# Eight column tiles ahead of each norm, head sums with the squares as stationary operand, and operands moved by 32 bytes

## The chip, the cores and the metric

The kernel runs on one NeuronCore of a Trainium2 chip. The metric is the device time of one execution in microseconds (us). The names used for engines: PE is TensorE's matmul stream and PEld its weight loads, DVE is VectorE, ACT is ScalarE, POOL is GpSimd, SP is SyncE, which here only issues transfers. SBUF is the on-chip memory, PSUM the accumulator memory, whose banks hold 512 float32 columns.

## What is computed

Two different blocks of two layers each, one after the other, on 256 tokens of width 1024. The first block's layer is, cut to what matters here:

```python
def hybrid_layer(x, ...):
    h = rms_norm(x, norm1_g)
    proj = h @ w_in
    q, k, v, iq, ik, iw, a_in, c_in, g_in = jnp.split(proj, IN_SPLITS, axis=-1)
    q = partial_rope(rms_norm(q.reshape(B, S, N_HEADS, HEAD_DIM), q_norm_g), *rope_attn)
    k = partial_rope(rms_norm(k.reshape(B, S, N_KV_HEADS, HEAD_DIM), k_norm_g), *rope_attn)
    y_attn = dsa_attention(q, k, v, iq, ik, iw) @ w_attn_out
    a_val, a_gate = jnp.split(a_in, 2, axis=-1)
    a = causal_dwconv(a_val * jax.nn.sigmoid(a_gate), conf_conv_w) + conf_conv_b
    ...
    x = x + merged @ w_o
    u = causal_dwconv(rms_norm(x, norm2_g) @ w_up, ffn_conv_w) + ffn_conv_b
    u_gate, u_val = jnp.split(u, 2, axis=-1)
    return x + (jax.nn.silu(u_gate) * u_val) @ w_down
```

The second block works on 512 rows (the 256 tokens and 256 context rows z); it also normalizes its query and key heads (of 64 elements) by the root of their mean square.

## The kernel before

Everything lies transposed in SBUF: 128 features on the partitions, tokens along the columns, a vector of 1024 features as eight slices `k`. Each matrix product is made one column tile (128 outputs) at a time in split precision. `Kern.weights` (L71 to L85) loads a tile of 128 x 1024 weights on SP's queue, ACT rounds it to float32r (`whi`, L68), and DVE or POOL subtracts to get the rest (`wlo`, L69); the operand is split in the same way into `hh` and `hl`. `Kern.mm` (L94 to L103) then issues 24 matmuls into a PSUM bank: per slice `whi` x `hh` (L100) and `whi` x `hl` (L101), and after them the eight of `wlo` x `hh` (L103). In the first block each matmul streams 256 columns, in most of the second block 512. In the first block's projections every second weight tile's subtraction goes to POOL, as one instruction of 1024 columns.

Before a norm, `early` (L205 to L212) splits x times the gain without the root, as soon as a slice of x is there (`oph`, `opl`). `opening` (L230 to L248) runs the first column tiles on that operand: four at the first norm of a layer (tag n1), three at the second (n2), each in a bank of its own. After the first tile it issues the two matmuls of the mean square (`mean`, L182) and the root (`rms`, L185 to L196), then makes the normed operand slice by slice (L242 and `split`), and multiplies each finished tile in PSUM by the root (L244). The following tiles use the normed operand. The sums for the root come from `sq_add` (L158 to L176): ACT squares, DVE adds.

The tiles are consumed in pairs: after n1 by a tanh on ACT (L291) and a product on DVE (L292) for the 31-tap convolution, whose taps (L275) DVE works off between other work; after n2 by a bias on ACT (L608) and two taps on DVE (L610), then a product (L614). A bank is free for the next tile when its consumers are done. Instructions run in order on each engine, in an order that a scheduler sets when the kernel is built; SP issues the weight loads in their order, up to four tiles ahead.

The mean squares of the ten key and query heads (`sums`, L340): ACT squares a tile, and one matmul with a 128 x 32 matrix that has a column of ones at the head's place streams the 256 squares, so that ten matmuls add rows to one bank. `head_rms` (L359) copies the 32 rows to SBUF (L361), transposes them (L364) and takes the root on 64 columns. The second block does the same with `hot2` (L1290) and `head_norms` (L993 to L1004).

At the start, x comes in four transfers on two queues, then the vectors of layer 0 (245 KB), an identity, the table const1 (864 KB) and the weights.

## Time and profile before

| | |
|---|---|
| median of three runs | 2914.49 us (2914.34 to 2915.78) |
| the profiled execution's own time | 2914.19 us |
| its span (first to last instruction) | 2912.4 us |
| PE busy | 2845.2 us, 98% |
| DVE busy | 2123.3 us, 73% |
| ACT busy | 1336.4 us, 46% |
| POOL busy | 351.1 us, 12% |
| the first block, by its last weight tiles | up to about 1180 us |

Busy time is what an engine's instructions cover; matmuls are pipelined, so a matmul's own duration is longer than its distance to the next one, and it is the distance that adds up. The chain that ended last follows the work back from the end, at each step to what released it.

### The profile page before, as it was taken

The numbers are of one execution on the slowest core, as the hardware profiler recorded it, in microseconds if no ns is written. First come the engines' busy times: TensorE is split into PE (matmuls) and PEld (weight loads), VectorE is DVE, ScalarE is ACT, GpSimd is POOL, SyncE is SP. The second block draws the span as 40 slices with busy tenths as digits, with TensorE's granted clock in tenths as the row PEclk, the third lists the DMA queues.
The fourth block names the chain that finished last, engine by engine and source line by source line (L and its number), as shares of the span: only waits on it lengthen the run. The fifth ranks groups of instructions, "written<-read, shape, count | busy, mean of one in ns | idle before, by whom it ended". The sixth has DMA issues, their size and how long they took to land.

```text
span 2912.4 us, 47602 instructions
## 1 busy us (share of the span) xinstructions
PE 2845.2 (98%) x18738; PEld 2551.3 (88%) x18738; DVE 2123.3 (73%) x3809; ACT 1336.4 (46%) x2189; POOL 351.1 (12%) x204
## 2 busy tenths in 40 slices
PE   7999999999899999999999999999999999999999
PEld 7889999998899999888888679888888888877999
DVE  7999789889986898666777855766765444585654
ACT  5455666544546765433226464433234332365543
POOL 3333422033234210000000000000000000000000
PEclk9999999999999999999999999999999999999999
DMA  6445557654455567554552112544644445422455
GB/s 209 145 127 162 177 186 219 226 173 137 136 160 176 182 217 239 165 155 161 182 183 97 53 45 73 159 145 148 188 142 152 137 136 167 134 88 68 167 180 154
DMA packets 127936, 447.65 MB, mean 154 GB/s; under 512 B 14304, under 2 KB 19936, under 8 KB 127072
## 3 DMA queue, kind: packets, MB, share of 16 engines
q1 hardware_dynamic: 124672, 439.14, 47.4%
q10 hardware_dynamic: 3040, 5.48, 0.5%
q8 instruction: 147, 2.41, 0.3%
q14 instruction: 77, 0.63, 0.1%
HBM read 443.51 MB, written 1.05 MB: 153 GB/s over the span
## 4 chain that ended last, share of the span: by engine, by line
PE 87%; DVE 8%; ACT 2%; DMA 1%; issue 1%; POOL 0%; SPq 0%; ACTq 0%; DVEq 0%; POOLq 0%
PE mmb L100 26%; PE mmb L101 26%; PE mmb L103 25%; DVE wlo L69 2%; PE outb L980 1%; PE atb L947 1%; ACT whi L68 1%; PE mmb L110 1%; PE mmb L111 1%; PE mmb L109 1%; DVE opl L69 1%; DVE cvb L275 1%; DMA mraw<-in_w_mod_dram 1%; PE mmb L975 1%; PE atb L182 0%
## 5 line engine op out<-in xcount | busy, mean ns | idle before, releaser
L68 ACT ACTIVATE whi<-wraw 128x1024 fp32r<-128x1024 f32 (+1 forms) x688 | 715.7, 1042 | 946.1 <-PE mmb L101 792.8
L69 DVE TENSOR_TENSOR wlo<-wraw,whi 128x1024 fp32r<-128x1024 f32 (+1 forms) x575 | 698.9, 1217 | 232.8 <-ACT whi L68 187.8
L100 PE MATMUL mmb<-oph,whi 128*128 128x256 f32 x2512 | 635.0, 290 | 20.6 <-ACT whi L68 11.9
L101 PE MATMUL mmb<-opl,whi 128*128 128x256 f32 x2512 | 629.2, 287 | 5.2 <-DVE opl L69 3.0
L100 PE MATMUL mmb<-hh,whi 128*128 128x512 f32 (+1 forms) x1776 | 612.4, 357 | 1.1 <-ACT whi L68 1.1
L101 PE MATMUL mmb<-hl,whi 128*128 128x512 f32 (+1 forms) x1776 | 609.2, 355 | 0.0
L100 PEld LDWEIGHTS mmb<-oph,whi 128*128 128x128 f32 x2512 | 486.6, 194 | 34.4 <-ACT whi L68 13.7
L101 PEld LDWEIGHTS mmb<-opl,whi 128*128 128x128 f32 x2512 | 487.0, 194 | 13.2 <-DVE opl L69 4.8
L777 DVE SCALAR_TENSOR_TENSOR mjunk<-mraw,cvec 128x1024 f32<-128x1024 f32 x256 | 316.0, 1234 | 245.1 <-DMA mraw<-in_w_mod_dram 238.6
L100 PEld LDWEIGHTS mmb<-hh,whi 128*128 128x128 f32 x1776 | 336.0, 189 | 55.4 <-issue 8.0
L103 PE MATMUL mmb<-hh,wlo 128*128 128x512 f32 (+1 forms) x1776 | 379.3, 355 | 0.0
L101 PEld LDWEIGHTS mmb<-hl,whi 128*128 128x128 f32 x1776 | 335.9, 189 | 47.4 <-issue 1.9
L103 PE MATMUL mmb<-oph,wlo 128*128 128x256 f32 x2512 | 357.1, 285 | 0.0
L100 PE MATMUL mmb<-dh,whi 128*128 128x256 f32 (+1 forms) x1122 | 343.2, 328 | 1.8 <-ACT whi L68 1.7
L69 POOL TENSOR_TENSOR wlo<-wraw,whi 128x1024 fp32r<-128x1024 f32 x113 | 285.8, 2529 | 487.5 <-ACT whi L68 402.7
L101 PE MATMUL mmb<-dl,whi 128*128 128x256 f32 (+1 forms) x1122 | 341.9, 327 | 0.0
L103 PEld LDWEIGHTS mmb<-hh,wlo 128*128 128x128 f32 x1776 | 297.9, 189 | 46.7 <-issue 0.4
L103 PEld LDWEIGHTS mmb<-oph,wlo 128*128 128x128 f32 x2512 | 327.5, 193 | 0.2
L100 PEld LDWEIGHTS mmb<-dh,whi 128*128 128x128 f32 x1122 | 213.2, 190 | 21.0 <-ACT whi L68 2.4
L101 PEld LDWEIGHTS mmb<-dl,whi 128*128 128x128 f32 x1122 | 213.3, 190 | 18.2
L275 DVE SCALAR_TENSOR_TENSOR cvb<-u,vec,cvb 128x256 f32<-128x256 f32 x480 | 212.6, 481 | 3.6
L103 PE MATMUL mmb<-dh,wlo 128*128 128x256 f32 (+1 forms) x1122 | 209.1, 327 | 0.2 <-DVE wlo L69 0.2
(335 smaller groups left out, 2838.4 us busy)
## 6 DMA issues: line engine op xcount, KB each, us to landing
wraw<-in_w_ff_dram SPq DMA_DIRECT2D x208, 512.0 KB, 3.5
wraw<-in_w_in_dram SPq DMA_DIRECT2D x200, 512.0 KB, 3.6
mraw<-in_w_mod_dram SPq DMA_DIRECT2D x144, 512.0 KB, 4.1
wraw<-in_w_up_dram SPq DMA_DIRECT2D x88, 512.0 KB, 4.3
wraw<-in_w_y_dram SPq DMA_DIRECT2D x64, 512.0 KB, 3.6
wraw<-in_w_ff_dram SPq DMA_DIRECT2D x64, 448.0 KB, 3.8
wraw<-in_w_down_dram SPq DMA_DIRECT2D x32, 448.0 KB, 4.0
wraw<-in_w_down_dram SPq DMA_DIRECT2D x16, 512.0 KB, 4.6
```

The costliest lines, as they stand in the source:

```text
L68: nc.scalar.activation(hi, src, AF.Copy)
L69: (lo_eng or nc.vector).tensor_tensor(lo, src, hi.bitcast(F32), op=OP.subtract)
L100: nc.tensor.matmul(ps, hi[:, k], xh[:, k0 + k], start=start and k == 0, stop=False)
L101: nc.tensor.matmul(ps, hi[:, k], xl[:, k0 + k], start=False, stop=False)
L103: nc.tensor.matmul(ps, lo[:, k], xh[:, k0 + k], start=False, stop=stop and k == kt - 1)
L109: nc.tensor.matmul(ps, hi[:, k], a, start=start, stop=False)
L110: nc.tensor.matmul(ps, hi[:, k], b, start=False, stop=False)
L111: nc.tensor.matmul(ps, lo[:, k], a, start=False, stop=stop)
L275: nc.vector.scalar_tensor_tensor(box[0], u[:, j, t:t + S], V("cw", 31 * j + t), box[0], op0=OP.mult, op1=OP.add)
L777: nc.vector.scalar_tensor_tensor(junk, raw, 1.0, K.cvec[:, e], op0=OP.mult, op1=OP.mult, accum_out=K.mods[l][:, e, 8 * m + k:8 * m + k + 1])
L947: nc.tensor.matmul(ps[:, :n], self.q[:, self.pair, tb * P:(tb + 1) * P], self.kpad[:, self.key(e), self.keys[0]:self.keys[1]], start=True, ...
L975: nc.tensor.transpose(pt[:, s * P:(s + 1) * P], lg[:, e, s * P:(s + 1) * P], K.ident)
```

## The change

- `opening` takes eight column tiles at every norm of the first block, in n banks (four at n1, five at n2), so that banks hold two tiles side by side. The first two tiles run slices 0 to 6 first, with the root's matmuls behind the first (behind the second at the very start), and both slices 7 come after that. The normed operand is made between the multiplications of the following tiles.
- The head sums: the squares (128 features x 128 tokens) become the stationary operand, a single column of 1/1024 streams; the result has tokens on the partitions at once. The copy and the transposes go, and the root is taken on 20 columns. The second block does the same with a 128 x 2 matrix: two or four matmuls where there was one.
- `shifted`: the float32r operands of the first block and those of the last feed-forward start 8 elements (32 bytes) into their tiles, at an odd multiple of 32 bytes; they started at multiples of 512 bytes. The weight tiles stay where they were, and so do the operands that stream 512 columns.
- POOL's subtraction is cut into four instructions of two slices.
- At the start the gains of the first norm (4 KB) are loaded by themselves ahead of x, the first weight tile is loaded in two halves between the parts of x, ACT loads its table for the copies at once, the squares come after all of `early`, and the other constants wait until the norm is made. z and the second block's vectors are loaded later.

```diff
     def weights(self, src, kt=KD):
+        return self.ahead.pop() if self.ahead else self.load(src, kt)
+
+    def load(self, src, kt=KD, cut=KD):
...
-        nc.sync.dma_start(raw[:, :kt], src)
+        cuts = [slice(k, min(k + cut, kt)) for k in range(0, kt, cut)]
+        for c in cuts:
+            nc.sync.dma_start(raw[:, c], src[:, c])
...
+            if self.nsplit % of < share:
+                for c in cuts:
+                    nc.scalar.activation(hi[:, c], raw[:, c], AF.Copy)
+                for k in range(0, kt, 2):
+                    c = slice(k, min(k + 2, kt))
+                    nc.gpsimd.tensor_tensor(lo[:, c], raw[:, c], hi[:, c].bitcast(F32), op=OP.subtract)
+            else:
+                for c in cuts:
+                    self.split(hi[:, c], lo[:, c], raw[:, c])
...
-        def opening(gname, srcs):
-            banks = []
-            for i, src in enumerate(srcs):
...
+        def opening(gname, srcs, n):
+            banks = [K.bank() for _ in range(n)]
+            tiles = [banks[i % n][:, i // n * S:(i // n + 1) * S] for i in range(len(srcs))]
+            two = []
+            for i in range(2):
+                two.append(K.weights(srcs[i]))
+                K.mm(tiles[i], two[i], *K.early, ks=range(KD - 1))
+                if i == (l == 0 and gname == "n1"):
                     rb = K.rms()
...
+            for i in range(2):
+                K.mm(tiles[i], two[i], *K.early, ks=(KD - 1,))
+            def finish(i):
+                if i > 1:
+                    K.mm(tiles[i], K.weights(srcs[i]), *K.early)
+                nc.vector.tensor_tensor(tiles[i], tiles[i], rb, op=OP.mult)
+            finish(0)
+            finish(1)
+            hh, hl = operand()
+            for k in range(KD):
+                if k % 3 == 2:
+                    finish(2 + k // 3)
+                h = K.np.tile([P, S], F32, name="hn", bufs=3)
+                nc.vector.scalar_tensor_tensor(h, x[:, k], V(gname, k), rb, op0=OP.mult, op1=OP.mult)
+                act = K.split(hh[:, k], hl[:, k], h)
+            for i in range(4, len(tiles)):
+                finish(i)
+            K.imm = (K.imm + len(srcs) - n) % len(K.mmset)
+            return tiles, hh, hl, act
...
             def sums(j, sq):
-                nc.tensor.matmul(ssq[0:32, :S], K.onehot[:, j], sq, start=j == 0, stop=j == 9)
+                for b in range(2):
+                    nc.tensor.matmul(ssq[:, 10 * b + j:10 * b + j + 1], sq[:, b * P:(b + 1) * P], K.inv[:, 0:1],
+                                     start=True, stop=True)
...
-            first, hh, hl = opening("n2", [A["w_up"][l, i] for i in range(3)])
+            first, hh, hl, _ = opening("n2", [A["w_up"][l, i] for i in range(8)], 5)
...
+            dh = shifted(ff, [NF, S], name="dh")
+            dl = shifted(ff, [NF, S], name="dl")
...
+def shifted(pool, shape, **kw):
+    n, w = shape
+    t = pool.tile([P, n * w + 16], F32R, **kw)
+    return t[:, 8:8 + n * w].rearrange("p (a b) -> p a b", b=w)
```

The order of the instructions at three places. On ACT at the start of the program, before:

```order
L211 ACT_TABLE_LOAD
L211 ACTIVATE oph<-xz,vec_0_69 128x256
L68 ACTIVATE whi<-wraw 128x1024
L163 ACTIVATE nacc_87<-xz 128x256
L211 ACTIVATE oph<-xz,vec_0_69 128x256
L166 ACTIVATE nsq<-xz 128x256
```

and in the change (the lines are those of the changed file):

```order
L683 ACT_TABLE_LOAD
L683 ACTIVATE nwarm<-inv 128x1
L68 ACTIVATE whi<-wraw 128x512
L228 ACTIVATE oph<-xz,vec_0_69 128x256
L68 ACTIVATE whi<-wraw 128x512
L228 ACTIVATE oph<-xz,vec_0_69 128x256 x5
L90 ACTIVATE whi<-wraw 128x1024
L228 ACTIVATE oph<-xz,vec_0_69 128x256 x2
L180 ACTIVATE nacc_112<-xz 128x256
L183 ACTIVATE nsq<-xz 128x256 x4
```

The table load no longer waits for data, the squares stand behind all eight slices of `oph`, and the second weight tile is rounded before them.

On DVE at the second norm of the first layer, where the first tiles are consumed, before (mmb_4726, mmb_4801 and mmb_4833 are the three tiles made ahead, nry the root, uu0 and uu1 the two halves of a consumed pair):

```order
L244 TENSOR_TENSOR mmb_4833<-mmb_4833,nry_4761 128x256
L610 SCALAR_TENSOR_TENSOR uu0_4871<-mmb_4726,vec1_0_69,uu0_4871 128x255
L610 SCALAR_TENSOR_TENSOR uu1_4875<-mmb_4801,vec1_0_69,uu1_4875 128x255
L610 SCALAR_TENSOR_TENSOR uu0_4871<-mmb_4726,vec1_0_69,uu0_4871 128x254
L610 SCALAR_TENSOR_TENSOR uu1_4875<-mmb_4801,vec1_0_69,uu1_4875 128x254
```

and in the change (mmb_4905 to mmb_4909 are the five banks; mmb_4908 holds tile 3 alone and is the first that the ninth tile can take):

```order
L638 SCALAR_TENSOR_TENSOR uu1_5211<-mmb_4906,vec1_0_69,uu1_5211 128x255
L638 SCALAR_TENSOR_TENSOR uu1_5223<-mmb_4908,vec1_0_69,uu1_5223 128x255
L264 TENSOR_TENSOR mmb_4907<-mmb_4907,nry_4941 128x256
L638 SCALAR_TENSOR_TENSOR uu1_5211<-mmb_4906,vec1_0_69,uu1_5211 128x254
L638 SCALAR_TENSOR_TENSOR uu1_5223<-mmb_4908,vec1_0_69,uu1_5223 128x254
L642 TENSOR_TENSOR uu0_5207<-uu0_5207,uu1_5211 128x256
```

The multiplication of the last tile (mmb_4907, which waits for that tile's matmuls) now stands ahead of the last reading of mmb_4908.

On PE at the end of the query heads of the first layer, before:

```order
L103 MATMUL mmb<-oph,wlo 128x256 x8
L341 MATMUL cvb<-sq,const_306 32x256
L100 MATMUL mmb<-oph,whi 128x256
L341 MATMUL cvb<-sq,const_306 32x256
L101 MATMUL mmb<-opl,whi 128x256
```

and in the change:

```order
L120 MATMUL mmb<-oph,wlo 128x256 x8
L376 MATMUL cvb<-inv,sq 128x1 x2
L117 MATMUL mmb<-oph,whi 128x256
L118 MATMUL mmb<-opl,whi 128x256
L117 MATMUL mmb<-oph,whi 128x256
L118 MATMUL mmb<-opl,whi 128x256
L376 MATMUL cvb<-inv,sq 128x1 x2
```

Two one-column matmuls stand where one of 256 columns stood, and the transposes L364 that came some matmuls later are gone.

## Rows read from the trace of the kernel before

**Rows 1.** The page: engines, then the chain that ended last, by engine.

```profile
PE 2845.2 (98%) x18738; PEld 2551.3 (88%) x18738; DVE 2123.3 (73%) x3809; ACT 1336.4 (46%) x2189; POOL 351.1 (12%) x204
...
PE 87%; DVE 8%; ACT 2%; DMA 1%; issue 1%; POOL 0%; SPq 0%; ACTq 0%; DVEq 0%; POOLq 0%
```

**Rows 2.** A stretch: length, busy PE PEld DVE ACT POOL, PE's clock, DMA.

```profile
410.00:570.00 160.00, 158.69 (x1315) 157.90 (x1314) 144.60 (x233) 100.79 (x160) 26.86 (x22) 1.00 0.67 212
```

**Rows 3.** Timeline: start, us, engine, line, count [idle before], at the start.

```profile
7.48 1.28 ACT L211 ACT_TABLE_LOAD   x1 [7.48 <-DMA vec<-in_vec_dram]
8.78 0.51 ACT L211 ACTIVATE oph<-xz,vec 128x256 fp32r<-128x256 f32 x1
10.78 1.06 ACT L68 ACTIVATE whi<-wraw 128x1024 fp32r<-128x1024 f32 x1 [1.50 <-DMA wraw<-in_w_in_dram]
...
24.18 1.12 PE L103 MATMUL mmb<-oph,wlo 128*128 128x256 f32 x8
25.14 0.28 PE L100 MATMUL mmb<-oph,whi 128*128 128x256 f32 x1
```

**Rows 4.** The tile xz in the first 20 us: its loads.

```profile
DMA to landing us min/median/max: 4.1/4.8/5.4
```

**Rows 5.** Timeline of PE: the waits at the openings of the four norms.

```profile
32.45 0.39 PE L100 MATMUL mmb<-oph,whi 128*128 128x256 f32 x1 [1.39 <-ACT th L291]
35.41 0.38 PE L100 MATMUL mmb<-oph,whi 128*128 128x256 f32 x1 [1.27 <-ACT oph L68]
...
400.00 0.35 PE L100 MATMUL mmb<-oph,whi 128*128 128x256 f32 x1 [0.61 <-DVE xz L575]
...
597.22 0.39 PE L101 MATMUL mmb<-opl,whi 128*128 128x256 f32 x1 [1.61 <-DVE opl L212]
610.07 0.38 PE L100 MATMUL mmb<-oph,whi 128*128 128x256 f32 x1 [2.02 <-ACT th L291]
...
976.50 0.36 PE L100 MATMUL mmb<-oph,whi 128*128 128x256 f32 x1 [0.87 <-DVE xz L575]
```

**Rows 6.** Groups by line and shape: count, busy us, mean ns, idle before.

```profile
L244 DVE TENSOR_TENSOR mmb<-mmb,nry 128x256 f32<-128x256 f32 x14 | 5.7, 421 | 0.0
L610 DVE SCALAR_TENSOR_TENSOR uu<-mmb,vec,uu 128x254 f32<-128x254 f32 x88 | 41.2, 476 | 1.0
L69 DVE TENSOR_TENSOR wlo<-wraw,whi 128x1024 fp32r<-128x1024 f32 x479 | 594.9, 1243 | 182.0 <-ACT whi L68 156.7 <-PE mmb L103 20.6 <-PE atb L1092 2.0
L69 POOL TENSOR_TENSOR wlo<-wraw,whi 128x1024 fp32r<-128x1024 f32 x113 | 285.8, 2529 | 487.5 <-ACT whi L68 402.7 <-DVE cvb L275 22.5 <-PE mmb L103 10.6
L69 POOL TENSOR_TENSOR dl<-uu,dh 128x256 fp32r<-128x256 f32 x44 | 50.9, 1156 | 236.9 <-ACT dh L68 236.9
L69 DVE TENSOR_TENSOR opl<-mg,oph 128x256 fp32r<-128x256 f32 x16 | 18.6, 1161 | 5.3 <-ACT oph L68 5.1
L69 DVE TENSOR_TENSOR opl<-hn,oph 128x256 fp32r<-128x256 f32 x32 | 13.9, 478 | 0.0
```

**Rows 7.** Timeline of PE: the last head sums of the first layer.

```profile
120.85 0.39 PE L100 MATMUL mmb<-oph,whi 128*128 128x256 f32 x1
121.16 0.62 PE L341 MATMUL cvb<-sq,const 128*32 128x256 f32 x2
121.71 0.39 PE L101 MATMUL mmb<-opl,whi 128*128 128x256 f32 x1
...
125.00 0.41 PE L364 MATMUL atb<-ident,ssr 32*128 32x32 f32 x2 [2.20 <-DVE ssr L361]
```

**Rows 8.** Timeline of PE: float32 matmuls of 64 columns, in the second block.

```profile
2669.78 2.00 PE L980 MATMUL outb<-av,pT 128*128 128x64 f32 x16
2671.62 1.08 PE L947 MATMUL atb<-nkp,nq 128*128 128x512 f32 x2
```

**Rows 9.** Timeline of PE: float32r matmuls of 512 columns, in the second block.

```profile
2193.45 1.98 PE L103 MATMUL mmb<-hh,wlo 128*128 128x512 f32 x8
2195.27 0.39 PE L100 MATMUL mmb<-hh,whi 128*128 128x512 f32 x1
```

More of the change, by code (lines that the diff above doesn't have):

```diff
@@ L52, in __init__ @@
         self.imm = self.iat = 0
-        self.acc, self.last = {}, {}
+        self.acc, self.last, self.ahead = {}, {}, []
     @contextmanager
@@ L206, in early @@
     if k == 0:
-        K.early = (pool.tile([P, KD, S], F32R, name="oph", tag="op2h"),
-                   pool.tile([P, KD, S], F32R, name="opl", tag="op2l"))
+        K.early = (shifted(pool, [KD, S], name="oph", tag="op2h"),
+                   shifted(pool, [KD, S], name="opl", tag="op2l"))
     hh, hl = K.early
@@ L223, in operand @@
         def operand(pool=big, tag="op0"):
[L224 to L225 removed]
+            return (shifted(pool, [KD, S], name="oph", tag=tag + "h"),
+                    shifted(pool, [KD, S], name="opl", tag=tag + "l"))
         def w_in(j):
             return K.weights(A["w_in"][l, j], KD)
[L230 to L246 removed]
+        def opening(gname, srcs, n):
[6 more added lines that the diff above has]
+                if i == (l == 0 and gname == "n1"):
+                    rb = K.rms()
+            for i in range(2):
[17 more added lines that the diff above has]
+            return tiles, hh, hl, act
@@ L615, in first_layer @@
                 K.split(dh[:, j], dl[:, j], us[0], nc.gpsimd)
+                if j == 0 and l == DEPTH - 1:
+                    with tc.issue_after(act.ins):
+                        nc.scalar.dma_start(xz[:, :, S:], A["z"])
+                        for i in range(DEPTH):
+                            nc.scalar.dma_start(vec2[i], A["vec2"][i])
                 if j == 2:
@@ L693, in const1_array @@
     causal = np.concatenate([tri, np.zeros((P, P), np.float32), tri], axis=1)
-    onehot = np.zeros((P, 10, 32), np.float32)
-    for h in range(10):
-        onehot[:, h, h] = 1.0
-    return np.ascontiguousarray(np.concatenate([acos, asin, icos, isin, causal, onehot.reshape(P, 320)], axis=1))
+    return np.ascontiguousarray(np.concatenate([acos, asin, icos, isin, causal], axis=1))
 def ptile(w):
@@ L870, in feed_forward @@
         pad(ff, PAD_FF2)
-        dh = ff.tile([P, NF, T], F32R, name="dh")
-        dl = ff.tile([P, NF, T], F32R, name="dl")
+        dh = shifted(ff, [NF, T], name="dh") if T == S else ff.tile([P, NF, T], F32R, name="dh")
+        dl = shifted(ff, [NF, T], name="dl") if T == S else ff.tile([P, NF, T], F32R, name="dl")
         for j in range(NF):
@@ L1526, in two_blocks_kernel @@
         early(K, big, xz[:, :, :S], vec1[0], "n1", k)
+    for k in range(KD):
         K.sq_add(xz[:, k, :S], k)
```

103 lines of the change are left out of this document (37 added, 66 removed).

## The prediction

> **What bounds the kernel now.** I read the page first: PE is busy for 98% of the span, and the chain that ended last runs 87% through PE and 8% through DVE [rows 1]. So time can come from three places only: from fewer or shorter matmuls, from gaps between them, and from what lies ahead of the first one. The stretches show where a wait of PE is likely: in the feed-forward of the first layer (410 to 570 us) PE works without a pause at full clock, but DVE is busy for 144.6 of 160 us beside it [rows 2]; there DVE has a tenth to spare, and an added DVE instruction can reach PE. The timeline gives distances, which count more than durations: eight float32r matmuls of 256 columns begin at 24.18 and the next at 25.14, so one takes 0.12 us [rows 3]; eight of 512 columns take 1.82 us, 0.2275 each [rows 9]. The 256 further columns cost 0.1075 us, so 0.0125 us of each matmul does not depend on its length. A column tile of 24 matmuls takes 2.9 us. The openings show small waits of PE [rows 5], the last head sums one long wait [rows 7].
>
> **The start.** Now ACT waits until 7.48 us for the vectors, loads its table for 1.28 us, and waits again for weights until 10.78 us; the third column tile begins at 25.14 us [rows 3]. In the change the table is loaded beforehand, and x, whose transfers land 4.1 to 5.4 us after issue [rows 4], comes with the first weights, without 245 KB of vectors and 864 KB of constants in the way. I let ACT begin near 6 us. Up to the third tile's weights it does two halves of a weight tile (0.6 us each, an estimate from 1.06), eight slices of `oph` at 0.51 [rows 3], a weight tile, eight squares (at most as long as `oph`, the same shape), a table load and one more weight tile: 1.2 + 4.1 + 1.1 + 4.1 + 1.3 + 1.1 = 12.9 us, so the third tile begins near 18.9 instead of 25.1. The first two tiles fit before it. I take **-6** us; bounds -8 (squares faster, loads earlier) and -2 (the loads crowd each other).
>
> **The first norm (n1) of each layer.** PE waits 1.39 and 1.27 us in layer 0, 1.61 and 2.02 in layer 1 [rows 5], for the last slice, for a bank and for the normed operand. Eight tiles last 23 us, longer than the normed operand needs, and slice 7 is put off behind two tiles; both waits go. Late next is a bank: the ninth tile needs the bank of tiles 0 and 4, which is free after the third product on DVE, and in the order these products stand behind the multiplication of the eighth tile: 0.42 us [rows 6] and three products of about 0.48 (as the tap of the same size, [rows 6]), 1.9 us, of which six or seven matmuls of another tile fill 0.8. So 2.7 becomes 1.1 and 3.6 becomes 1.1: **-4** us; bounds -6 and 0.
>
> **The second norm (n2).** Here there is little to gain: 0.61 and 0.87 us [rows 5]. The order puts the multiplication of the eighth tile ahead of the last reading of the bank that the ninth tile takes: 0.42 + 2 x 0.48 = 1.4 us of wait. Then DVE has four consumed pairs in arrears, with a subtraction of 1.24 us per weight tile between them [rows 6], and the tenth and the twelfth tile wait about 1 us each. DVE also does 18 more multiplications over the four norms (32 instead of 14), 7.6 us, with a tenth of its time free [rows 2]. I put 3.2 us of waits against 0.7 at each of the two norms: **+5** us; bounds 0 and +10. Queued behind these DVE instructions are the subtractions of the next weight tiles, so PE would wait for `wlo` too.
>
> **Head sums.** A sum of 256 columns takes 0.55 us from its start to PE's next matmul [rows 7]. The new pair of matmuls streams one column, and its price is that of loading 128 x 128 float32 weights: not in the trace with one column; the nearest row is 64 columns, 16 records in 1.84 us, 0.115 each [rows 8]. A float32 product makes two records, so a head costs 4 x 0.115 = 0.46 us: 20 x 0.09 = -1.8 us. The transposes go, with the wait of 2.20 us for DVE's copy in layer 0 [rows 7] and 0.3 us of their own in each layer: -2.8. The root's chain is shorter by copy and transposes, which only moves the next wait earlier. Together **-4.6** us; bounds -7 and 0 (the wait reappears at the next transposes, for the same DVE). In the second block 48 small products of 0.23 us (11 us) stand for 14 long ones of about the same sum; 16 transposes and two copies per call go: **-2** us, bounds -5 and +2.
>
> **POOL in four pieces.** A subtraction of 128 x 256 on DVE takes 0.48 us where POOL rests and 1.16 us on average where POOL works on weights [rows 6]: it stands still until POOL's 2.53 us end. With pieces it stands still for less. A piece cost 1.16 us in the feed-forward [rows 6], four of them 4.6 us against 2.53 now, while PE needs 5.8 us for the two tiles of which POOL has one; POOL stays in time, and PE may begin with the first piece. Of 16 x 0.68 = 11 us in this one group I let a third come through: **-4** us; bounds -10 and +6 (POOL late).
>
> **The shift by 32 bytes.** It touches 3 x 2512 matmuls on the first block's operands and 3 x 528 on the shifted `dh` and `dl`: 9120 of 18,000. No row has a float32r stream that starts there. Best case: the 0.0125 us that do not depend on length go, -114 us. Worst: 32 bytes are 8 columns, and a first piece used in part costs as much time as these, 8 x 0.42 ns = 3.4 ns, +31 us. I take **0**, since the 0.12 us of the nearest rows is the same in every phase, whatever else runs, so nothing shows a conflict that a shift would resolve. The Trainium skill ("SBUF — State Buffer", Specifications) gives SBUF lines of 16 bytes; a start at a multiple of 32 begins a line like any other, which would make the shift worth nothing either way. No run here shows that yet; by it the sum is the one below.
>
> **The sum.** -6 - 4 + 5 - 4.6 - 2 - 4 = -15.6 us from the profiled execution's 2914.2 us: 2898.6, rounded to **2899**. The median of the runs is 2914.5, so nothing has to be corrected. 0.2% is 5.8 us, about what a measurement can tell from no change.
>
> **The rivals.**
> - *The shift makes the matmuls quicker.* For it: 0.0125 us per matmul that no column explains; a loss in the fetching of operands would look so. Against it: 512 columns have the same loss, and their operands stay unshifted. All of it would give 2899 - 114 = 2785; with DVE at nine tenths [rows 2] I would expect a quarter of it to be lost, 2813, and with half the loss removed 2848. The Trainium skill ("TensorE: Matmul & The Clock Gate", Back-to-back issue gap) puts the warm distance at N/2.4 + 2.5 ns, 109 ns here, where the trace has 120; were the shift to bring it there, the estimate would be 2899 - 100 = 2799.
> - *The waits only move.* The n2 norms cost +10 instead of +5, and sums and POOL give nothing: -6 - 4 + 10 = 0, 2914. For it: the order of DVE at n2, and DVE's narrow margin [rows 2]. Against it: the wait of 2.20 us [rows 7] has its cause removed.
> - *The shift makes the matmuls dearer*, and the kernel slower: +31 - 15.6, 2930. Place: every matmul of the first block. It decides from 15.6 us / 9120 = 1.7 ns per matmul. For it: a stream that starts off a multiple of 64 bytes touches one more unit of that size (17 instead of 16). Against it: no row.
> - That the change doesn't cover what it should is part of the second: the early tiles then wait for banks instead of for the norm.
>
> **How the numbers follow.** Forecast 0.45, quicker matmuls 0.33, moved waits 0.12, dearer matmuls 0.10. The range reaches down to 2815, about the strongest form of the first rival after DVE's share, and up to 2914, the second rival; left out are the dearer matmuls and the extreme of the first, under 2 in 10. The forecast's own range, from the bounds of its terms taken two thirds as far, is 2888 to 2910. Faster by over 0.2%: nearly all of forecast and first rival plus a little, 0.79; within 0.2%: 0.12; slower: 0.09.
>
> **What would show it.** Distance of the matmuls on `oph`, 0.120 us: 0.117 or less speaks for the first rival, 0.122 or more for the third. The third tile should begin at 18 to 20 us. At n1 one wait near 1 us for a DVE product should stand where two stood; at n2 waits of 1 to 2 us for taps on DVE. No wait before the transposes of the key norm longer than now. POOL's pieces near 0.75 to 1.2 us, and the subtractions of 128 x 256 on DVE below 0.9 us on average. I am wrong if the distance changes at all, since 1 ns of it is worth 9 us, more than any single wait above.

## The result, and the profile after

The change made the kernel faster by three times what was forecast: 2869.16 us median (2867.26 to 2869.87, four runs) against 2914.41 us before, a ratio of 0.9843 with a 95% interval of 0.9826 to 0.986. That is 45.3 us less, where the prediction said 15.5 less. The range given (2815 to 2914) holds the time, the size does not fit. All times in this document are of undisturbed executions; one of the four of run e7 was disturbed (4105 us) and is left out.

The page of the changed kernel, engines and then the chain that ended last, the lines that answer to [rows 1]:

```profile
PE 2810.7 (98%) x18826; PEld 2545.4 (89%) x18826; DVE 2081.8 (73%) x3818; ACT 1338.7 (47%) x2193; POOL 423.8 (15%) x543
...
PE 85%; DVE 9%; ACT 2%; issue 2%; DMA 1%; POOL 0%; ACTq 0%; SPq 0%; DVEq 0%
```

Nothing has changed in kind: PE bounds the kernel. Its gaps and its distances have to be compared place by place. I followed the end of each column tile (the eighth matmul of `wlo`) through both traces: by the third tile the change is 6.5 us ahead, behind the sixth product of the first convolution 9.5, at the end of layer 0's attention 25, at the start of its second norm 29, behind that norm 25, then 37 behind the index scores of layer 1, 45 ahead of its second norm, 40 behind it, 41 at the start of the second block, and 44 at the end of the program.

The start, timeline of ACT and then of PE in the changed kernel (start, us, engine, line, idle before):

```profile
2.29 1.28 ACT L683 ACT_TABLE_LOAD   x1 [2.29 <-issue]
...
6.93 0.63 ACT L68 ACTIVATE whi<-wraw 128x512 fp32r<-128x512 f32 x1 [3.14 <-DMA wraw<-in_w_in_dram]
7.47 0.49 ACT L228 ACTIVATE oph<-xz,vec 128x256 fp32r<-128x256 f32 x1
...
16.22 1.04 ACT L68 ACTIVATE whi<-wraw 128x1024 fp32r<-128x1024 f32 x1
```

```profile
13.56 0.41 PE L118 MATMUL mmb<-opl,whi 128*128 128x256 f32 x1
13.77 1.27 PE L120 MATMUL mmb<-oph,wlo 128*128 128x256 f32 x7
...
17.97 0.59 PE L199 MATMUL atb<-nsq,inv 128*128 128x256 f32 x2
...
18.75 0.28 PE L118 MATMUL mmb<-opl,whi 128*128 128x256 f32 x1
...
20.54 1.12 PE L120 MATMUL mmb<-oph,wlo 128*128 128x256 f32 x8
21.49 0.28 PE L117 MATMUL mmb<-oph,whi 128*128 128x256 f32 x1
```

The third tile begins one matmul ahead of the row at 18.75, at 18.64 us, where the prediction said 18.9 and [rows 3] had 25.1. ACT was done with that tile's weights at 17.26 us (the row at 16.22). What came last was PE itself, with its first two tiles, whose matmuls stood 0.21 us apart up to 13.8 us, and with the root's matmuls (L199).

The waits of PE at the openings, n1 of layer 0, n2 of layer 0 (three rows), n1 of layer 1 and n2 of layer 1, the answer to [rows 5]:

```profile
37.36 0.38 PE L117 MATMUL mmb<-oph,whi 128*128 128x256 f32 x1 [1.49 <-ACT th L325]
...
396.81 0.36 PE L117 MATMUL mmb<-oph,whi 128*128 128x256 f32 x1 [1.81 <-DVE uu L638]
401.16 0.36 PE L117 MATMUL mmb<-oph,whi 128*128 128x256 f32 x1 [1.25 <-DVE uu L638]
407.98 0.36 PE L117 MATMUL mmb<-oph,whi 128*128 128x256 f32 x1 [0.88 <-DVE uu L638]
...
594.08 0.39 PE L117 MATMUL mmb<-oph,whi 128*128 128x256 f32 x1 [2.42 <-ACT th L325]
...
960.09 0.55 PE L117 MATMUL mmb<-oph,whi 128*128 128x256 f32 x1 [4.93 <-DVE uu L638]
```

At n2 PE waits for a tap on DVE, as forecast, but 3.9 us in all in layer 0 and 4.9 us at once in layer 1, where I had put 3.2 at each. At n1 the waits are 1.49 and 2.42 us, and a tanh on ACT ends both, not a product on DVE.

The granted clock shows what the prediction did not look for. Before, the windows (length, busy PE PEld DVE ACT POOL, PE's clock, DMA) behind three of PE's waits:

```profile
126.00:130.00 4.00, 4.00 (x21) 4.00 (x21) 2.10 (x8) 1.44 (x2) 0.00 (x0) 0.50 0.23 92
...
162.00:166.00 4.00, 3.13 (x10) 2.77 (x11) 4.00 (x5) 1.48 (x5) 1.33 (x1) 0.51 0.33 114
...
736.00:740.00 4.00, 3.24 (x11) 2.88 (x12) 4.00 (x10) 1.97 (x6) 0.00 (x0) 0.50 0.01 4
```

These are the stretches behind the wait of 2.20 us for the head sums' copy [rows 7] and behind two waits ahead of the index scores. The first of those is this row, still of the kernel before:

```profile
162.87 2.07 PE L414 MATMUL atb<-ikb,iq 128*128 128x256 f32 x4 [4.25 <-ACT vn L399]
```

From 126 to 130 us PE works without a pause and at 1.2 GHz all the same, half its speed. One minus the clock, times 4 us, summed over all windows of 4 us up to 1180 us, gives 13.7 us lost before in the profiled execution. In the changed kernel the same places read:

```profile
98.00:114.00 16.00, 16.00 (x138) 16.00 (x137) 13.38 (x33) 8.04 (x15) 5.65 (x8) 1.00 0.56 166
114.00:134.00 20.00, 19.07 (x162) 18.87 (x162) 20.00 (x36) 7.94 (x12) 11.99 (x15) 1.00 0.50 154
134.00:150.00 16.00, 13.34 (x107) 12.93 (x106) 16.00 (x34) 7.74 (x14) 8.11 (x10) 1.00 0.41 135
...
700.00:704.00 4.00, 3.27 (x11) 2.90 (x12) 4.00 (x9) 1.70 (x5) 0.00 (x0) 0.57 0.82 236
```

Layer 0's attention now runs at full clock, and the same sum is 5.1 us, 8.6 less. That compares one execution with one, and executions of the same kernel differ: the granted clock of whole executions lies between 0.992 and 0.997 in the 41 runs of the kernel before for which it is on record, 0.9942 on average, and averages 0.9953 in the four of the change. Over the span that is some 3 us, an estimate (the clock is recorded to 0.001, 2.9 us of a run). So the clock gave back some 3 to 9 of the 45 us.

Groups after, to set beside [rows 6] (count, busy us, mean ns, idle before):

```profile
L94 POOL TENSOR_TENSOR wlo<-wraw,whi 128x256 fp32r<-128x256 f32 x452 | 362.0, 831 | 392.8 <-ACT whi L90 360.4 <-DVE cvb L309 15.4 <-PE atb L502 6.3
...
L264 DVE TENSOR_TENSOR mmb<-mmb,nry 128x256 f32<-128x256 f32 x32 | 12.9, 424 | 0.0
L69 DVE TENSOR_TENSOR opl<-mg,oph 128x256 fp32r<-128x256 f32 x16 | 9.2, 572 | 4.8 <-ACT oph L68 4.4
```

The subtraction of the merged operand on DVE went from 1161 to 572 ns, and a piece on POOL takes 831 ns, both as forecast.

### The profile page after: what moved, and what is told of

Read it like the earlier page. It is cut to its first block, busy times and chain, and to the rows that moved or that the text cites. A ratio compares the mean times of both kernels' runs of the same rounds, so it can differ in the third digit from the quotient of the medians.

```text
span 2867.6 us, 48219 instructions
## 1 busy us (share of the span) xinstructions
PE 2810.7 (98%) x18826; PEld 2545.4 (89%) x18826; DVE 2081.8 (73%) x3818; ACT 1338.7 (47%) x2193; POOL 423.8 (15%) x543
## 3 DMA queue, kind: packets, MB, share of 16 engines
q8 instruction: 148, 2.42, 0.3%
## 4 chain that ended last, share of the span: by engine, by line
PE 85%; DVE 9%; ACT 2%; issue 2%; DMA 1%; POOL 0%; ACTq 0%; SPq 0%; DVEq 0%
PE mmb L117 25%; PE mmb L118 25%; PE mmb L120 25%; DVE wlo L69 3%; PE outb L1013 1%; PE atb L980 1%; PE mmb L127 1%; PE mmb L128 1%; PE mmb L126 1%; DVE cvb L309 1%; DMA mraw<-in_w_mod_dram 1%; ACT whi L68 1%; DVE uu L638 1%; PE mmb L1008 1%; DVE ia L449 1%
## 5 line engine op out<-in xcount | busy, mean ns | idle before, releaser
L68 ACT ACTIVATE whi<-wraw 128x1024 fp32r<-128x1024 f32 (+2 forms) x576 | 597.2, 1038 | 843.0 <-PE mmb L118 750.3
L69 DVE TENSOR_TENSOR wlo<-wraw,whi 128x1024 fp32r<-128x1024 f32 (+2 forms) x576 | 699.0, 1215 | 242.6 <-ACT whi L68 179.7
L117 PE MATMUL mmb<-oph,whi 128*128 128x256 f32 x2512 | 626.7, 287 | 23.3 <-DVE uu L638 8.9
L118 PE MATMUL mmb<-opl,whi 128*128 128x256 f32 x2512 | 620.4, 283 | 0.3
L117 PEld LDWEIGHTS mmb<-oph,whi 128*128 128x128 f32 x2512 | 475.9, 190 | 28.4 <-ACT oph L228 8.0
L118 PEld LDWEIGHTS mmb<-opl,whi 128*128 128x128 f32 x2512 | 478.2, 190 | 4.5 <-issue 2.9
L94 POOL TENSOR_TENSOR wlo<-wraw,whi 128x256 fp32r<-128x256 f32 x452 | 362.0, 831 | 392.8 <-ACT whi L90 360.4
L117 PEld LDWEIGHTS mmb<-hh,whi 128*128 128x128 f32 x1776 | 336.8, 190 | 49.6 <-issue 2.5
L120 PE MATMUL mmb<-oph,wlo 128*128 128x256 f32 x2512 | 351.2, 281 | 0.0
L120 PEld LDWEIGHTS mmb<-oph,wlo 128*128 128x128 f32 x2512 | 320.3, 188 | 0.3 <-issue 0.2
```

The source lines that it names most:

```text
L68: act = nc.scalar.activation(hi, src, AF.Copy)
L69: (lo_eng or nc.vector).tensor_tensor(lo, src, hi.bitcast(F32), op=OP.subtract)
L94: nc.gpsimd.tensor_tensor(lo[:, c], raw[:, c], hi[:, c].bitcast(F32), op=OP.subtract)
L117: nc.tensor.matmul(ps, hi[:, k], xh[:, k0 + k], start=start and k == 0, stop=False)
L118: nc.tensor.matmul(ps, hi[:, k], xl[:, k0 + k], start=False, stop=False)
L120: nc.tensor.matmul(ps, lo[:, k], xh[:, k0 + k], start=False, stop=stop and k == kt - 1)
```

## The experiments

Ratios are to the kernel before on the same chip, with 95% intervals; a difference between kernels measured at different times is the difference of their ratios times 2914.4 us. Each interval reaches some 5 us to either side, so such a difference is good to some 7 us (an estimate). The edit of e7 is in e11 as well, on another kernel.

| run | the kernel | median us | ratio |
|---|---|---|---|
| e1 | change, operands at their tiles' start | 2870.0 | 0.9845 [0.9831, 0.986] |
| e2 | change, 16 bytes in | 2863.8 | 0.9824 [0.9808, 0.9841] |
| e3 | change, 64 bytes in | 2861.8 | 0.9817 [0.9803, 0.9832] |
| e4 | before, shifted by 32 bytes | 2910.8 | 0.9988 [0.9979, 0.9997] |
| e5 | change, plain tiles | 2878.4 | 0.9881 [0.9864, 0.9897] |
| e6 | change, old head sums (first block) | 2878.8 | 0.9878 [0.9863, 0.9893] |
| e7 | change, POOL uncut | 2894.3 | 0.9933 [0.9916, 0.995] |
| e8 | change, three tiles at n2 | 2860.5 | 0.9818 [0.9803, 0.9832] |
| e9 | before, POOL in four pieces | 2890.8 | 0.9913 [0.9896, 0.9929] |
| e10 | change, POOL in two pieces | 2879.9 | 0.9872 [0.9857, 0.9887] |
| e11 | e8, POOL uncut | 2893.1 | 0.9914 [0.9898, 0.993] |
| e12 | e8, 64 bytes in | 2855.8 | 0.979 [0.9774, 0.9805] |
| e13 | change, all operands at the same 64 bytes | 2863.9 | 0.9819 [0.9804, 0.9833] |
| e14 | change, all at the same 192 bytes | 2853.3 | 0.9785 [0.9769, 0.9802] |
| e15 | change, four tiles at n1 | 2867.5 | 0.9831 [0.9816, 0.9846] |
| e16 | e12, POOL in eight pieces | 2846.9 | 0.9761 [0.9746, 0.9775] |
| e17 | e8, eight pieces, all at 192 bytes | 2842.2 | 0.9754 [0.9737, 0.977] |
| e18 | e17, second block's operands too | 2859.0 | 0.9815 [0.9801, 0.983] |

### Where the operands start (e1 to e5, e13, e14, e18)

In the first four runs the offset inside `shifted` is another, and e4 puts `shifted` into the kernel before:

```diff
-    return t[:, 8:8 + n * w].rearrange("p (a b) -> p a b", b=w)
+    return t[:, 0:n * w].rearrange("p (a b) -> p a b", b=w)
```

(e1; 4 in e2 and 16 in e3.)

> The changed kernel with the operands moved back to the start of their tiles (multiples of 64 bytes); the rest as changed. Theory A: the start of an operand sets part of each matmul's distance. Then the 256-column matmuls on oph, opl and dh stand 119.9 ns apart again, where the changed kernel has 118 to 119, and the time rises by about 9120 x 1.2 = 11 us, to about 2880. Rival: the distances became shorter because POOL reads and writes SBUF in smaller pieces, or because other work moved; then they stay at 118 to 119 ns without the shift and the time stays within 3 us of 2869.

> The changed kernel with the operands 16 bytes into their tiles instead of 32. Theory A in the form that any start off a multiple of 64 bytes helps: distances as in the changed kernel (118 to 119 ns), time 2866 to 2872. Rival form, that it has to be the half of 64 bytes: 119.9 ns and about 2880. A third form, that a start off a multiple of 32 costs a further piece: above 120 ns, over 2890.

> The changed kernel with the operands 64 bytes into their tiles instead of 32. If the remainder of 64 bytes decides: as without the shift, 119.9 ns and about 2880. If it is the distance to the weights' start, which lies at a multiple of 512 bytes, in larger units (128 bytes or more): 118 to 119 ns for the operands that land at an odd multiple of 64, and a time between 2869 and 2880.

> The kernel before with the shift by 32 bytes alone. Theory A: distances of 118 to 119 ns on the shifted operands and about 9120 x 1.2 = 11 us less, 2901 to 2906. Rival: the shift shortens nothing by itself, 119.9 ns and 2912 to 2917. If other engines' waits fill what PE saves, the distances fall but the time stays above 2908.

The mean distance of matmuls on `oph` and `opl`, over those between 100 and 150 ns, was 119.9 ns before, 118.5 in the change, 118.8 in e1, 118.0 in e2, 116.7 in e3 and 118.4 in e4. So it changed at all, and theory A in its first form fell: without the 32 bytes it did not go back, and the time did not either. The form by the remainder of 64 bytes fell with e3, whose operands start at multiples of 64 and are the quickest of these. What e1 still has of the change are the 64 bytes that each tile is longer by: by the addresses of the built program `opl` lies 64 bytes off a multiple of 128 there, and most `oph` 128 off a multiple of 512. In e4 the shorter distances are there, worth some 13 us (9120 x 1.5 ns), and 4.6 us come out of it. In its profile PE's idle time behind the first 30 us, gaps of over 150 ns summed, is 53.1 us against 49.6 before, and over its ten runs the granted clock averages 0.9917, against 0.9938 in the thirteen runs of the kernel before beside it, some 6 us by estimate. So what the matmuls save there goes mostly into waits and low clock.

> The changed kernel with plain operand tiles, as before: no shift and no 64 bytes more per tile, so that the operands lie at multiples of 256 bytes again. The theory so far: without the shift by 32 bytes the distances stayed short, so it is the starts of successive operands relative to each other that set the distance, not the start within 64 bytes; then here all 256-column matmuls stand 119.9 ns apart again and the time lies 5 to 12 us above 2869, at 2874 to 2881. Rival: the distances are short because of the rest of the change; then they stay at 118 to 119 ns and the time within 2 us of 2869.

```diff
-    t = pool.tile([P, n * w + 16], F32R, **kw)
-    return t[:, 8:8 + n * w].rearrange("p (a b) -> p a b", b=w)
+    return pool.tile([P, n, w], F32R, **kw)
```

With plain tiles the distance is 119.9 ns again and the time 9 us higher (11 by the ratios): this is the operands' part of the change. Eight matmuls of `wlo` and the one behind them, timeline of PE, first e5 and then the change (0.96 and 0.94 us for eight):

```profile
330.83 1.12 PE L120 MATMUL mmb<-oph,wlo 128*128 128x256 f32 x8
331.79 0.28 PE L117 MATMUL mmb<-oph,whi 128*128 128x256 f32 x1
```

```profile
331.25 1.10 PE L120 MATMUL mmb<-oph,wlo 128*128 128x256 f32 x8
332.19 0.28 PE L117 MATMUL mmb<-oph,whi 128*128 128x256 f32 x1
```

The next two tell whether it is their place relative to each other. Each tile gets 512 bytes more and the operands of all start 64 or 192 bytes in, so that they lie to each other as before, and only their place against multiples of 256 bytes is new; the weights start at multiples of 512:

```diff
-    t = pool.tile([P, n * w + 16], F32R, **kw)
-    return t[:, 8:8 + n * w].rearrange("p (a b) -> p a b", b=w)
+    t = pool.tile([P, n * w + 128], F32R, **kw)
+    return t[:, 48:48 + n * w].rearrange("p (a b) -> p a b", b=w)
```

(e14; 16 in e13.)

> The changed kernel with every shifted operand at 64 bytes behind a multiple of 256, all alike, so that successive operands lie at the same remainder as in the kernel before, and only the distance to the weights' starts (multiples of 512) is new. Theory B, the relation of an operand to the one before it: 119.9 ns and the 2878 of the plain tiles. Theory C, the relation to the weights: 116 to 118.5 ns, 2860 to 2870.

> The same with 192 bytes. Theory B: 119.9 ns, 2878. Theory C: with the operands 64 bytes in, the matmuls of wlo on those oph that lay at 192 stood 114.3 ns apart, the shortest of all; with every operand there all three kinds would come to 114 to 116, which is 9120 x 3 to 4 = 27 to 36 us off the changed kernel's distances; with a third of that lost in other waits 2845 to 2853. If only the wlo matmuls gain: 2860 to 2866.

Theory B fell: 117.6 ns in e13 and 115.2 in e14. The relation to the weights (theory C) is not shown by that alone, because no run moved the weights: the operand's own address would explain these two runs as well. e14 is 17 us faster than the change by the ratios. Its timeline has 0.91 us for eight:

```profile
327.35 1.07 PE L120 MATMUL mmb<-oph,wlo 128*128 128x256 f32 x8
328.26 0.28 PE L117 MATMUL mmb<-oph,whi 128*128 128x256 f32 x1
```

> The same with the operands of the second block, hh, hl and the hidden ones of its feed-forward, 192 bytes in as well, those of 512 columns among them. 256 columns: 2472 matmuls at 4 to 5 ns less, 10 to 12 us. 512 columns: 4938 matmuls; if the gain is one of each matmul's beginning, another 4 to 5 ns each, 20 to 25 us, together 2803 to 2812; if it grows with the columns, twice that, 2780 to 2790; if long matmuls gain nothing, 2826 to 2830.

```diff
-                K.hh = op.tile([P, KD, T2], F32R, name="hh")
-                K.hl = op.tile([P, KD, T2], F32R, name="hl")
+                K.hh = shifted(op, [KD, T2], name="hh")
+                K.hl = shifted(op, [KD, T2], name="hl")
...
-        dh = shifted(ff, [NF, T], name="dh") if T == S else ff.tile([P, NF, T], F32R, name="dh")
-        dl = shifted(ff, [NF, T], name="dl") if T == S else ff.tile([P, NF, T], F32R, name="dl")
+        dh = shifted(ff, [NF, T], name="dh")
+        dl = shifted(ff, [NF, T], name="dl")
```

All forms of the expectation missed: 16.7 us slower than e17. The second block's matmuls of 256 columns did go from 119.9 to 114.3 ns, but those of 512 columns from 227.1 to 233.3 for `hh` and `hl`. Timeline of PE, eight of 512 columns, 1.87 us where [rows 9] had 1.82:

```profile
1984.66 2.03 PE L120 MATMUL mmb<-hh,wlo 128*128 128x512 f32 x8
1986.53 0.39 PE L117 MATMUL mmb<-hh,whi 128*128 128x512 f32 x1
```

4938 x 6 ns = 30 us more against 2472 x 5.5 = 14 less: that is the 16. The start that helps a matmul of 256 columns costs one of 512.

### POOL's pieces (e7, e9, e10, e11, e16)

> The changed kernel with POOL's subtraction of a weight tile as one instruction of 1024 columns. Theory: one long instruction of POOL holds up whatever DVE does beside it, and what comes back are the waits of PE before the index scores (4.8 and 5.7 us before, 2.9 and 4.0 now) and at the last slices of the merged operand (1.7, 1.3 and 1.4 us before): up by 7 to 11 us, to 2876 to 2880. The prediction said 4 us: 2873. Rival: these waits went with the head sums; then within 2 us of 2869.

```diff
-                for k in range(0, kt, 2):
-                    c = slice(k, min(k + 2, kt))
-                    nc.gpsimd.tensor_tensor(lo[:, c], raw[:, c], hi[:, c].bitcast(F32), op=OP.subtract)
+                nc.gpsimd.tensor_tensor(lo[:, :kt], raw[:, :kt], hi[:, :kt].bitcast(F32), op=OP.subtract)
```

25.1 us came back, over twice the most that I expected. This is the largest part of the change. e9 asks for it the other way round, in the kernel before:

```diff
-            self.split(hi[:, :kt], lo[:, :kt], raw[:, :kt], eng)
+            if self.nsplit % of < share:
+                nc.scalar.activation(hi[:, :kt], raw[:, :kt], AF.Copy)
+                for k in range(0, kt, 2):
+                    c = slice(k, min(k + 2, kt))
+                    nc.gpsimd.tensor_tensor(lo[:, c], raw[:, c], hi[:, c].bitcast(F32), op=OP.subtract)
+            else:
+                self.split(hi[:, :kt], lo[:, :kt], raw[:, :kt])
```

> The kernel before with POOL's subtraction in four pieces alone. Uncut it cost the changed kernel 25.6 us where the prediction gave 4 and the waits in the profile 7 to 11. Theory: the waits that a held-up DVE makes for PE cost twice, since the granted clock falls behind them (before: 0.50 at 126 to 130, 162 to 166 and 736 to 740 us; a dip costs some 3.4 us by its windows). With pieces the waits before the index scores (4.8 and 5.7 us) shrink to 3 to 4, those on the merged operand go, and dips go with them; the waits for the head sums' copy stay. Then 10 to 16 us less: 2897 to 2903. Rival (the prediction's price): 2908 to 2911. Rival, that the pieces are worth as much here as in the changed kernel: 2885 to 2889.

2890.75 us, 25.3 less: cutting alone is worth as much in the old kernel, more than half of the whole change. Its profile says how, the group on DVE and two windows of attention in layer 0:

```profile
L69 DVE TENSOR_TENSOR opl<-mg,oph 128x256 fp32r<-128x256 f32 x16 | 9.1, 570 | 4.7 <-ACT oph L68 4.4
```

```profile
122.00:130.00 8.00, 8.00 (x67) 7.83 (x66) 7.04 (x24) 3.15 (x5) 3.13 (x6) 1.00 0.46 131
150.00:170.00 20.00, 17.63 (x128) 15.95 (x126) 20.00 (x48) 10.88 (x18) 10.26 (x12) 1.00 0.52 169
```

The wait of 2.20 us for the head sums' copy [rows 7] is gone with the old head sums still in place. Tile by tile, e9 gains 4.0 us there, 4.6 at the index scores of layer 0, 2.9 at the key norm and 1.6 at the index scores of layer 1, 1.3 to 1.7 at each of six other places; at the first norm of layer 1 it loses 3.3. The sum over windows of 4 us puts the loss to low clock at 6.9 us against 13.7 before, so 6.8 of the 25 us are clock; the granted clock of all runs gives about the same (0.9965 in e9, 0.9940 in the runs beside it, some 7 us by estimate). The rest is waits: PE's idle time, summed as for e4, is 33.9 us against 49.6, 15.7 less. The matmuls themselves did not change, their distance is 119.9 ns in both. What the cause looks like uncut, DVE and then POOL of the kernel before:

```profile
152.70 3.42 DVE L69 TENSOR_TENSOR wlo<-wraw,whi 128x1024 fp32r<-128x1024 f32 x1
```

```profile
152.03 3.01 POOL L69 TENSOR_TENSOR wlo<-wraw,whi 128x1024 fp32r<-128x1024 f32 x1 [0.74 <-ACT whi L68]
```

DVE's instruction takes 1.24 us on average [rows 6]; this one begins while POOL's runs and ends 1.1 us behind it. The Trainium skill ("SBUF — State Buffer", SBUF: two separate sides) says that a GpSimd instruction that reads SBUF and a DVE instruction with two SBUF inputs exclude each other and that the one that begins first keeps the port to its end; these rows agree. Not all of DVE is held up: the 480 taps of the 31-tap convolution (L275), which have one input in PSUM, take 457 to 491 ns in the same kernel.

> The changed kernel with POOL's subtraction in two pieces of four slices instead of four of two. If it is the length of one POOL instruction that holds up DVE, half of the way is lost: between 2873 and 2884, and DVE's subtractions of 128 x 256 on the merged operand lie between 0.5 and 1.16 us on average. If it is only that PE may begin with the first piece, 2870 to 2873. If any uncut piece over 1 us spoils it: near 2890.

> The kernel with three tiles ahead of the second norm (2860.5 us), with POOL's subtraction as one instruction. POOL takes no weight tiles at the second norm, so the two should add: 2860.5 + 25.6 = 2886, 2882 to 2890. Its profile should show where the 25 us lie: by the theory the waits before the index scores and of the merged operand are back at 4 to 6 and 1 to 2 us, and behind them the granted clock is down to 0.5 in three to five stretches, for 10 to 14 us together; the windows between 100 and 210 and between 690 and 800 us tell it. Rival: the clock stays at 1.0 and PE waits for wlo from POOL all through the projections.

```diff
-                for k in range(0, kt, 2):
-                    c = slice(k, min(k + 2, kt))
+                for k in range(0, kt, 4):
+                    c = slice(k, min(k + 4, kt))
```

(e10; e11 has e7's edit on e8.) Half the cutting gave more than half of it: of the 25 us, 14 come with two pieces by the medians (of 26, 18 by the ratios, with e10 8.5 us above the change). e11 lies 28 us above e8. The group on DVE, first e10 and then e11:

```profile
L69 DVE TENSOR_TENSOR opl<-mg,oph 128x256 fp32r<-128x256 f32 x16 | 11.7, 730 | 5.2 <-ACT oph L68 5.0
```

```profile
L69 DVE TENSOR_TENSOR opl<-mg,oph 128x256 fp32r<-128x256 f32 x16 | 17.3, 1081 | 5.2 <-ACT oph L68 5.1
```

One, two and four pieces give 1081, 730 and 572 ns for the same instruction. In e11 two windows show the low clock:

```profile
714.00:718.00 4.00, 0.44 (x1) 0.44 (x2) 4.00 (x8) 1.45 (x4) 0.10 (x1) 0.61 0.49 148
756.00:760.00 4.00, 3.28 (x13) 2.98 (x14) 4.00 (x15) 1.99 (x7) 0.18 (x1) 0.50 0.70 223
```

By windows of 4 us e11 loses 17.1 us to it and e8 1.7, 15 of the 28 us, some of it while PE stood still; the granted clock of all runs (0.9913 and 0.9968) gives some 16 by estimate. PE's idle time is 50.9 us against 36.0, another 15. So a wait that DVE's hold-up makes for PE is paid twice, as a wait and in the clock behind it. The rival, PE waiting for POOL's `wlo` throughout, fell: all the idle time ahead of the `wlo` matmuls of e11's first block is 0.8 us, and DVE ends it; in the kernel before it is 0.0.

> The kernel with three tiles ahead of the second norm and operands 64 bytes in (2855.8), with POOL's subtraction in eight pieces of one slice. From one to two to four pieces the changed kernel went 2894.7, 2879.9, 2869.2. If the length of one POOL instruction goes on counting: some 5 us less, 2849 to 2853. If a piece's fixed cost makes POOL late for PE: 2857 or more. If other waits lead by now: 2853 to 2857.

e16 came out 8.5 us under e12 (by the ratios), more than expected. The edit is e10's with 1 in place of 4. A piece of one slice costs 567 ns (512.7 us for 904), so POOL works 4.5 us for a tile, and for the first time PE waits for it:

```profile
L120 PE MATMUL mmb<-oph,wlo 128*128 128x256 f32 x2512 | 345.6, 279 | 2.9 <-POOL wlo L94 1.4 <-DVE wlo L69 0.9 <-POOL yv L531 0.6
```

### Head sums (e6)

> The changed kernel with the head sums of the first block as before (one matmul of 256 columns with the column of ones, a copy, two transposes, the root on 64 columns). My prediction gave these sums 4.6 us; the profile reads about 17 us between the first head and the tiles behind the last (9.0 and 7.9 in the two layers). Theory: shorter matmuls (0.27 us for each of 20 heads) and the chain to the root account for most of it; the time rises by 12 to 17 us, to 2881 to 2886. Rival: most of those waits went for another reason (POOL's pieces); then the time rises by 5 to 7 us only, to 2874 to 2876.

The edit puts back the matmul of 256 columns, the copy, two transposes and 64 columns:

```diff
-                for b in range(2):
-                    nc.tensor.matmul(ssq[:, 10 * b + j:10 * b + j + 1], sq[:, b * P:(b + 1) * P], K.inv[:, 0:1],
-                                     start=True, stop=True)
+                nc.tensor.matmul(ssq[0:32, :S], K.onehot[:, j], sq, start=j == 0, stop=j == 9)
```

9.6 us slower (10.2 by the ratios): between theory and rival. Of the 17 us that I read from the change's profile at this place, the rest belongs to POOL, as e9 shows. Timeline of PE, one head in the change:

```profile
80.64 0.50 PE L376 MATMUL cvb<-inv,sq 128*128 128x1 f32 x4
81.01 0.36 PE L117 MATMUL mmb<-oph,whi 128*128 128x256 f32 x1
```

0.37 us for a head against 0.55 [rows 7], so 20 x 0.18 = 3.6 us. What the other 6 us are is open. By windows of 4 us e6 loses 13.6 us to low clock and the change 5.1, but the granted clock of all runs averages 0.9950 and 0.9953, less than 1 us apart, and kernels that differ in other things also vary by several us in that sum (e1 8.5, e3 13.7). The wait of 2.20 us [rows 7] is none of it: e6 has the copy and the transposes again, and no wait of PE stands there.

### Tiles ahead (e8, e15)

> The changed kernel with three column tiles ahead of the second norm, as before, in place of eight; the first norm stays. The profile reads 8.8 us lost at the two second norms. Theory: the waits at the eighth and later tiles go and 0.6 to 0.9 us at each norm come back: 2860 to 2863. Rival: DVE is behind in this stretch whatever the order, and PE waits for it a few tiles later; then 2866 to 2870.

> The changed kernel with four column tiles ahead of the first norm, as before, in place of eight. The prediction gave the eight 4 us, the profile reads 3.6 for both layers (2.8 and 0.7): 2872 to 2874. Rival: as at the second norm, eight are too many and DVE's multiplications cost more than the waits they remove: 2863 to 2868.

```diff
-            first, hh, hl, _ = opening("n2", [A["w_up"][l, i] for i in range(8)], 5)
+            first, hh, hl, _ = opening("n2", [A["w_up"][l, i] for i in range(3)], 3)
```

(e15 has 4 in place of 8 at n1; both also leave out the calls for tiles that are no longer there.) At n2 the eight tiles cost 7 to 9 us, as the theory of e8 had it. ACT and DVE of the change at n2 of layer 1 show why it is more than the multiplications:

```profile
952.58 1.28 ACT L641 ACT_TABLE_LOAD   x1
...
956.52 1.06 ACTq L648 DMA_DIRECT2D vec<-in_vec_dram  x2
957.63 1.93 ACT L636 ACTIVATE uu<-mmb,vec 128x256 f32<-128x256 f32 x4 [0.70 <-issue]
```

```profile
958.23 2.50 DVE L638 SCALAR_TENSOR_TENSOR uu<-mmb,vec,uu 128x255 f32<-128x255 f32 x6 [1.75 <-ACT uu L636]
```

DVE stands idle for 1.75 us ahead of the tap that PE waits for: the tap needs ACT's bias (L636), and in front of that on ACT stand a table load and the issues of z's and the vectors' transfers, which the change had moved here. No run took these out by themselves; e8 has them too, and with three tiles its longest wait there is 0.87 us. At n1 four tiles are 1.6 us quicker by the medians and 3.5 by the ratios, within the intervals: eight gain nothing there that a run can show. Place by place they are 2.4 us ahead of e15 behind the norm of layer 0 and level with it (0.3 us) behind that of layer 1.

### Together (e12, e17)

> The two edits that were faster than the change, together: operands 64 bytes into their tiles (2861.8) and three tiles ahead of the second norm (2860.5). If they add: 2869.2 - 7.4 - 8.7 = 2853, 2849 to 2857. If DVE takes back what PE saves in the feed-forward: 2858 to 2861.

> Three tiles ahead of the second norm, POOL's subtraction in eight pieces and all shifted operands 192 bytes in, together. By adding: 2846.9 (the kernel with eight pieces, operands at 64 bytes) less 8.5 (2861.8 to 2853.3, the step from 64 to the same 192 for all): 2838. If waits on DVE take part of it back: 2840 to 2845.

e12 lies 8 us under each of the two that it joins by the ratios and adds nearly in full. e17 is the fastest, 0.9754 [0.9737, 0.977], 72 us less than before and 26 less than the change, 4 above what adding gave. Its interval meets that of e16, so whether 192 bytes still pay there stays open.

## Why the prediction was right and wrong

The direction was right. Two steps failed, and together they are the missing 30 us: POOL's pieces were priced at 4 us and the shift at nothing.

- **The start, -6:** right in size, 6.5, and by luck to 0.3 us: the third tile begins at 18.64 us for 18.9, but the step let ACT come last. ACT began at 6.93 instead of 6, needed 10.3 us instead of 12.9, and was done 1.6 us early; PE's first two tiles, which "fit before it", did not.
- **The first norm, -4:** not borne out. The waits that stand there are 1.49 and 2.42 us where the step had 1.1 each, a tanh on ACT ends them and not the product on DVE, and e15 finds no gain in eight tiles over four.
- **The second norm, +5:** right in sign and in the wait named, too small: 7 to 9 us (e8). The step priced DVE alone and left out ACT's table load and the issue of the moved transfers, which count on the queue that they are moved to; the rows show that for layer 1, and how much of its 4.9 us it is was not measured.
- **Head sums, -4.6:** 10 us (e6). A head saves 0.18 us, not 0.09: the price was taken from 64 columns, 0.115 us a record, and four records of one column take 0.37 together. The 2.20 us that the step counted for the copy were POOL's: that wait is gone in e6 and e9, which both keep the copy. The rest is open.
- **The second block, -2:** the place by place comparison has 41 us at its start and 44 at its end; no run took it alone.
- **POOL in four pieces, -4:** the mechanism was right and the size off by six: 25 us (e7, e9). The failing step was "Of 16 x 0.68 = 11 us in this one group I let a third come through". It counted the stall of one group alone, and no clock. Other DVE instructions that meet POOL's long one are held up as well, `wlo` of the next tile among them (3.42 us), PE then waits in the attention (e9's places), and some 7 (e9) to 16 us (e11) are the clock behind those waits.
- **The shift, 0:** wrong by 9 to 11 us (e5), and by the prediction's own sign, "if the distance changes at all": 118.5 ns for 119.9. The failing step was "since the 0.12 us of the nearest rows is the same in every phase, whatever else runs, so nothing shows a conflict that a shift would resolve". All those rows had operand and weights at multiples of 512 bytes, so their sameness could not tell. The Trainium skill ("SBUF — State Buffer", Specifications) gives lines of 16 bytes, from which I took that a start at 32 would be worth nothing either way; the measurement decides against that reading, for at starts that are all multiples of 16 the distances came to 115 to 120 ns. The first rival was right in kind and far too large, its mildest form 51 us. The 109 ns, an estimate for 256 columns from the formula in the Trainium skill ("TensorE: Matmul & The Clock Gate", Back-to-back issue gap), no run reached; 113.4 was the shortest.
- **The clock:** the step that is missing altogether. The sum priced a wait of PE at its length. The windows of the kernel before show 27 us at 1.2 GHz behind such waits, a loss of 13.7. POOL's pieces alone gave some 7 of them back (e9), the shift alone cost some 6 (e4), and for the whole change the runs leave some 3 to 9 us, which stand in no term.
- **Two sums** do not come out. Half of 114 us would have given 2842, or 2856 with a quarter of it lost, not 2848; and the bounds of the terms, two thirds as far, give 2885 to 2920, not 2888 to 2910. Neither moves the time that was forecast.

Taking each part out gave 9 to 11 (operands), 10 (head sums), 26 (POOL) and -7 to -9 us (second norm); with the start at 6.5 and some 3 us in the second block that makes 46 to 50 where 45 were measured. The parts share some waits, so the sum need not close.

## What to carry to other kernels

Before leaving work to GpSimd beside a busy VectorE, look in the groups for a VectorE instruction whose mean lies far above its like elsewhere, and cut GpSimd's instruction until it comes down; what it holds up may sit on quite another chain. A wait of TensorE is not priced until the granted clock behind it has been read as well. A distance that is the same to the nanosecond in all rows is no sign of a floor when all rows share their addresses: move one operand and measure, for each length of matmul by itself.

## What the runs showed that I had not expected

The distance of float32r matmuls depends on where the streamed operand starts. With the weights at multiples of 512 bytes and 256 columns it was 119.9 ns with the operands at multiples of 256 bytes, 117.6 with the operands 64 bytes and 115.2 with them 192 bytes further; with 512 columns 192 bytes made it 233.3 in place of 227.1. Whether it is the distance to the weights or the operand's own address that counts, why the two lengths go opposite ways, and why distances that were nearly all 120 spread over 112 to 128 once the operands are moved, is not settled: no run moved the weights. The shortest kind, `dh` at 192 bytes behind a multiple of 512 in e14, stood 113.4 ns apart.
